# Running the low half of a causal score tile over all 128 rows of TensorE

## The chip, the cores and the metric

The kernel runs on one core of one Trainium2 chip. The metric is the device time of one execution in microseconds (us), taken as the median of several runs. A profile of one execution gives every instruction's start and duration on TensorE's matmuls (PE), TensorE's weight loads (PEld), VectorE (DVE), ScalarE (ACT), GpSimd (POOL) and the DMA issues of SyncE (SP).

## The reference

One decoder layer for 512 positions and 1024 channels in float32. Three mixers read the same normalised input: a gated short convolution, causal attention with 8 heads of 64 channels, and attention over 256 memory tokens. A gated merge, an output projection and an MLP with a convolution follow. The change lies in the causal attention, whose scores are

```python
qh = rmsnorm(q.reshape(bsz, s, h, 64), moba_q_gain)      # h = 8 heads of 64 channels
kh = rmsnorm(k.reshape(bsz, s, h, 64), moba_k_gain)
scores = einsum('qhd,khd->hqk', qh, kh) * 64 ** -0.5     # causal: key <= query
out = softmax(scores) @ vh                               # two blocks of 256: all earlier ones are selected
```

## The kernel before

Every product is made in a reduced float32 format of TensorE (float32r). To keep the accuracy, each operand is cut into a high part (ScalarE copies it into the reduced format) and a low part (VectorE subtracts the high part from the original). An ordinary product is then three matmuls into one PSUM bank, in `mm3` (L235 to L237): high times high, low times high, high times low. The weights arrive as 512 KB pieces of eight 128x128 blocks, through three buffers `raw` that SP loads (L180); ScalarE (L197, `hi`) and VectorE (L200, `lo`) cut them two pieces ahead of their use.

Most of the time goes into projections of 128x128 weight blocks against 512 positions. Attention runs beside them as background tasks: generators that emit their next step after a given number of half tiles (12 matmuls each) have passed on TensorE. TensorE's order is exactly the order of the program. For ScalarE, VectorE, GpSimd and SP a planner orders the instructions after the start of the kernel, from its own model of the times. The causal heads are spawned 7 or 8 half tiles apart.

Heads come in pairs p, because a tile of 128 channels holds two heads of 64. For a pair, the normalised queries are split once into high and low (L242 on ScalarE, L244 on VectorE). Three DMAs of 128 KB from SP (L677) then lay the high queries of head 0 into both halves of one tile and those of head 1 into both halves of another. The keys of a head go into one tile `k2` (written `k` in the profile's rows): the high keys on the head's own 64 partitions (L680), the low keys on the other 64 (L681). So one matmul over 128 rows sums high keys times high queries and low keys times high queries (L689). A second matmul adds high keys times low queries (L690): it uses only the head's own 64 rows of `k2` and of the tile of low queries.

The scores of a head are four tiles t of 128 keys, over 512, 384, 256 and 256 queries, in two banks of the tag "s". Two tiles are emitted, one half tile of other work is let pass, and then come the other two. ScalarE copies each out (L692); mask, maximum, exponential and split follow on GpSimd, VectorE and ScalarE. Six half tiles later the products with the values begin (L748): for two key tiles at a time, each with its high and its low probabilities, over the same 512, 384, 256 and 256 queries, all over 128 rows.

Tiles of queries and `k2` come from the tag "st" with 8 buffers; a buffer is free again when its last reader is done.

Of the kernel before, what the change touches and what calls it, by code (L numbers as in the profile page):

```python
# [26 lines left out]

# The start of the kernel: its pieces of work in the order in which ScalarE, VectorE and TensorE
# take them up.  Each word begins a piece or carries it on to its next step, mostly from its
# ScalarE half to its VectorE half.  c: cut weight piece; x, m: split chunk of x, of mem;  # L30
# q, n: add up its squares; R, N: row factors of x, of mem;
# Q: memory queries from a chunk of x; s: their row factors; K, V: memory keys, values;
# h: chunk of the normalised x; C: first projection of the conv mixer.
PLAN = """
# [7 lines left out]

# Packed per-channel vectors: name -> (first column, columns).
VEC = {}
# [10 lines left out]

# Column tiles of w_in.
T_B, T_C, T_X, T_Q, T_K, T_V, T_QM, T_G = 0, 4, 8, 12, 16, 20, 24, 28


def weight_units():  # L60
    """The 128x128 weight blocks (matrix, row chunk, column chunk) in the order of use."""
    u = []

    def inner(m, c, nk):
        u.extend((m, k, c) for k in range(nk))

    def outer(m, cs, nk):
        u.extend((m, k, c) for k in range(nk) for c in cs)

    outer("w_in", range(T_QM, T_QM + 4), KD)  # L70
    for c in range(4):
        inner("w_mem_kv", c, KD)
    outer("w_mem_kv", range(4, 8), KD)
    for c in range(4):
        for t in (T_C, T_X, T_B):
            inner("w_in", t + c, KD)
    for p in range(4):
        if p == 3:
            outer("w_in", range(T_V, T_V + 4), KD)
        inner("w_in", T_Q + p, KD)  # L80
        inner("w_in", T_K + p, KD)
    for g, m, ahead in ((0, "w_br_conv", 0), (2, "w_br_mem", 0), (1, "w_br_moba", AHEAD)):
        n = max(ahead, 1)
        for j in range(n):
            inner("w_in", T_G + 8 * g + j, KD)
        for j in range(8):
            inner(m, j, 4)
            if n + j < 8:
                inner("w_in", T_G + 8 * g + n + j, KD)
    outer("w_o", range(4), KD)  # L90
    for c in range(4, 8):
        inner("w_o", c, KD)
    outer("w_up", (0, NF, 1, NF + 1), KD)
    for f in range(2, NF):
        inner("w_up", f, KD)
        inner("w_up", NF + f, KD)
    outer("w_down", range(4), NF)
    for c in range(4, 8):
        inner("w_down", c, NF)
    return u  # L100
# [10 lines left out]
def layer_kernel(ctx: ExitStack, tc: tile.TileContext, xT, memT, vecs, ws, outT):  # L111
# [14 lines left out]
    def nm(s):  # L126
        count[0] += 1
        return f"{s}_{count[0]}"
# [8 lines left out]

# [1 line left out]
    warm = cp.tile([P, ML], FR, name="warm")  # L139
# [12 lines left out]

# [1 line left out]
    tasks = []  # L154
# [13 lines left out]

# [1 line left out]
    st = {"u": 0, "left": 0, "off": 0, "loaded": 0, "dram": 0, "cut": 0, "use": 0, "n": 0, "look": 0}  # L170
# [36 lines left out]
    def take(want, n=1):  # L207
        """The next n blocks (in one piece) as (high, low) parts."""
        for i in range(n):
            assert units[st["u"] + i] == want[i], (units[st["u"] + i], want[i])  # L210
        if st["left"] == 0:
            i = st["use"]
            st["use"] = i + 1
            while st["cut"] <= min(i + st["look"], len(sizes) - 1):
                cut_piece()
            while st["loaded"] < min(st["cut"] + 2, len(sizes)):
                load_piece()
            cuts.pop(i - 1, None)
            st["left"], st["off"] = sizes[i], 0
        assert st["left"] >= n  # L220
        hi, lo = cuts[st["use"] - 1]
        o = st["off"] * P
        st["off"] += n
        st["left"] -= n
        st["u"] += n
        return hi[:, o : o + n * P], lo[:, o : o + n * P]
# [25 lines left out]
    def split(dst, src, scale=None):  # L252
        """dst = (high, low) of src, or of src * scale."""
        for _ in split_steps(dst, src, scale):
            pass
# [23 lines left out]
    def fold(dst, src, op):  # L279
        """dst[32 a + j, b] = the 32 rows 32 a + i of src's column 32 b + j, put together."""  # L280
        nc.vector.tensor_reduce(  # L281
            dst, src.rearrange("p (b i) -> p b i", i=32), axis=AX.X, op=op, apply_transpose=True
        )

    def spread(dst, src):
        """dst[32 a + i, 32 b + j] = src[32 a + j, b]."""
        n = src.shape[-1]
        nc.vector.transpose(
            dst.rearrange("p (b i) -> p b i", i=32),
            src.unsqueeze(2).to_broadcast([src.shape[0], n, 32]),  # L290
        )

    def join_steps(part, op, width=P, act=True):
        """Put a fold's quadrants together, over all or over each half of the partitions."""
        def shift(n):
# [22 lines left out]
    def root_steps(w, v):  # L318
        """w = (v + EPS) ** -0.5: ScalarE's seed with a Newton step."""
        s = small(v.shape[-1])  # L320
# [15 lines left out]
    def row_steps(out, w, mean):  # L336
        """The row factors from the channels' shares of the mean squares."""
        part = small(mean.shape[-1] // 32)
# [8 lines left out]
    def head_norm(q, gain, wait):  # L347
        """RMS norm of q over the 128 channels of its head, in place."""
        n = q.shape[-1]
# [10 lines left out]

    # ================= mixers =================
    mid = ctx.enter_context(ExitStack())
# [4 lines left out]

# [1 line left out]
    start = ExitStack()  # L369
# [7 lines left out]

# [1 line left out]
    xr, mraw, xs = [], [], []  # L379
# [19 lines left out]
    rb = cp.tile([P, S], F32, name="rb")  # L399
    spots = [("st", 8)] * 8 + [("ph", 4)] * 3 + [("pl", 4)] * 3 + [("S", 2)] * 2  # L400
    spots = iter(spots)
# [4 lines left out]

    # The tensor engine's clock rises while it waits for the first loads.
    junk = bank("s")
# [118 lines left out]

# [1 line left out]
    y_mem = []  # L529

    def mem_head(i):
        qh = (
            sp.tile([P, S], FR, tag="st", name=nm("qmh"), bufs=8),
            sp.tile([P, S], FR, tag="st", name=nm("qml"), bufs=8),
        )
# [41 lines left out]

# [1 line left out]
    def conv3(u, w, b):  # L579
        """Causal width-3 taps over u, whose first two columns are the zero padding."""  # L580
        t = tmp()
# [6 lines left out]
    for c in range(4):  # L588
        # The first tile runs from x, whose row factors come in here, while h is finished.
        src = xs if c == 0 else hx  # L590
# [21 lines left out]

# [1 line left out]
    qkn = [[None, None] for _ in range(4)]  # L614
# [46 lines left out]

    # query columns that key tile t serves, and where they lie in a packed row
    OFF = (0, 512, 896, 1152)
    pairs, qs = {}, {}

    def moba_head(h):
        p, j = divmod(h, 2)
        own, oth = halves(j)
        kn = qkn[p][1][own, :]
        if j == 0:  # L670
            qs[p] = tuple(
                sp.tile([P, S], FR, tag="st", name=nm(n), bufs=8) for n in ("qh", "qh", "ql")
            )
            a, b, lo = qs[p]
            split((a, lo), qkn[p][0])
            for dst, src in ((b[own, :], a[oth, :]), (b[oth, :], a[oth, :]), (a[oth, :], a[own, :])):
                nc.sync.dma_start(dst.bitcast(F32), src.bitcast(F32))  # L677
        q_hi, q_lo = qs[p][j], qs[p][2][own, :]
        k2 = sp.tile([P, S], FR, tag="st", name=nm("k2"), bufs=8)
        nc.scalar.activation(k2[own, :], kn, AF.Copy)  # L680
# [3 lines left out]
        for t in range(4):  # L684
# [4 lines left out]
            nc.tensor.matmul(acc[:, :n], l, q_hi[:, q0:], start=True, stop=False)  # L689
            nc.tensor.matmul(acc[:, :n], l[own, :], q_lo[:, q0:], start=False, stop=True)  # L690
            w = S - P * t
# [77 lines left out]

# [1 line left out]
    merged = [None] * 8  # L771
# [60 lines left out]

# [1 line left out]
    x2, h2 = [], []  # L834
# [21 lines left out]

    # ================= MLP =================
    fp = ctx.enter_context(tc.tile_pool(name="fp", bufs=2 * NF))
# [36 lines left out]
    for c in range(4, 7):  # L895
        finish(proj_inner("w_down", c, mlp, tag="s"), c)
    # The last tile ends in two halves, so that less of it is left to store at the end.
    parts = [(bank(), slice(0, S // 2)), (bank(), slice(S // 2, S))]
# [61 lines left out]
```

## Time and profile before

| what | value |
|---|---|
| median of 3 runs | 856.29 us (854.37 to 857.18) |
| span of the profiled execution | 854.7 us |
| PE busy | 848.1 us (99%) in 3714 matmuls |
| PEld busy | 682.4 us (80%) in 3714 loads |
| DVE busy | 519.7 us (61%) |
| ACT busy | 381.3 us (45%) |
| POOL busy | 46.6 us (5%) |
| DMA moved | 86.19 MB, mean 101 GB/s |
| granted TensorE clock, mean | 0.998 of full speed |

The page of the profile gives the span of the profiled execution and no time of its own beside it; the span lies inside the range of the three runs. A busy share tells how long an engine had something in it: matmuls overlap in the array, so a matmul's duration is longer than the step from its start to the next one's start, and a PE that is busy throughout may still step slowly. The steps between starts are what to read.

### The profile page before, as it was taken

How to read it: one execution, taken by the hardware profiler on the slowest of the kernel's cores; microseconds unless marked ns; L12 is line 12 of the kernel's file. 1: busy time of each engine (PE TensorE's matmuls, PEld its weight loads, DVE VectorE, ACT ScalarE, POOL GpSimd, SP SyncE). 2: the span in 40 equal slices, each digit the busy share in tenths (PEclk: the TensorE clock that was granted, in tenths of full speed). 3: DMA queues.
4: the chain of work that ended last, by engine and by line, in shares of the span. 5: the costliest groups of instructions: out<-in, count | busy, mean ns of one | idle time of the engine just before them, and what ended most of it. 6: DMA issues, size and time to landing. Idle time of an engine off the chain costs nothing.

```text
span 854.7 us, 9970 instructions
## 1 busy us (share of the span) xinstructions
PE 848.1 (99%) x3714; PEld 682.4 (80%) x3714; DVE 519.7 (61%) x834; ACT 381.3 (45%) x682; POOL 46.6 (5%) x97
## 2 busy tenths in 40 slices
PE   9999999999999999999999999999999999999998
PEld 7788888877777777778888888888888888888888
DVE  5997898947756776656456666556655556323221
ACT  6666767736645654444334443333333333211110
POOL 0200000101211011110000000000000000000000
PEclk9999999999999999999999999999999999999999
DMA  8353222332322222225222222332223322233410
GB/s 297 116 173 104 79 96 78 109 101 75 93 75 93 99 74 79 73 81 187 98 99 98 80 94 99 99 98 83 91 99 98 99 99 79 94 99 120 139 62 25
DMA packets 25633, 86.19 MB, mean 101 GB/s; under 512 B 2928, under 2 KB 3568, under 8 KB 25456
## 3 DMA queue, kind: packets, MB, share of 16 engines
q1 hardware_dynamic: 25440, 85.47, 30.2%
q8 instruction: 29, 0.48, 0.2%
q14 instruction: 20, 0.16, 0.1%
q10 hardware_dynamic: 144, 0.08, 0.0%
HBM read 81.87 MB, written 2.10 MB: 98 GB/s over the span
## 4 chain that ended last, share of the span: by engine, by line
PE 95%; DVE 2%; DMA 2%; issue 0%; ACT 0%; SPq 0%; DVEq 0%; ACTq 0%
PE acc L235 25%; PE acc L237 24%; PE acc L236 24%; PE s L236 6%; PE s L237 6%; PE s L235 6%; PE s L690 1%; PE m L748 1%; DMA raw<-ws 1%; PE s L689 1%; DMA xr<-xT 1%; DVE mh L248 0%; DVE lo L200 0%; DVE ss_x L433 0%; PE m L237 0%
## 5 line engine op out<-in xcount | busy, mean ns | idle before, releaser
L200 DVE TENSOR_TENSOR lo<-raw,hi 128x1024 fp32r<-128x1024 f32 (+1 forms) x148 | 179.0, 1211 | 157.7 <-ACT hi L197 157.4
L197 ACT ACTIVATE hi<-raw 128x1024 fp32r<-128x1024 f32 (+1 forms) x148 | 154.9, 1047 | 267.9 <-PE acc L237 158.2
L235 PE MATMUL acc<-h,hi 128*128 128x512 f32 x568 | 225.6, 397 | 0.0
L237 PE MATMUL acc<-h,hi 128*128 128x512 f32 x568 | 224.3, 395 | 0.0
L236 PE MATMUL acc<-h,lo 128*128 128x512 f32 x568 | 224.2, 395 | 0.0
L235 PEld LDWEIGHTS acc<-h,hi 128*128 128x128 f32 x568 | 106.7, 188 | 26.5 <-issue 0.9
L237 PEld LDWEIGHTS acc<-h,hi 128*128 128x128 f32 x568 | 106.7, 188 | 25.7
L236 PEld LDWEIGHTS acc<-h,lo 128*128 128x128 f32 x568 | 106.8, 188 | 24.8
L236 PE MATMUL acc<-m,lo 128*128 128x512 f32 (+1 forms) x132 | 47.1, 357 | 0.0
L235 PE MATMUL acc<-m,hi 128*128 128x512 f32 (+1 forms) x132 | 47.1, 357 | 0.0
L237 PE MATMUL acc<-m,hi 128*128 128x512 f32 (+1 forms) x132 | 47.1, 357 | 0.0
L235 PE MATMUL s<-h,hi 128*128 128x512 f32 x112 | 44.2, 395 | 0.0
L236 PE MATMUL s<-h,lo 128*128 128x512 f32 x112 | 44.2, 395 | 0.0
L237 PE MATMUL s<-h,hi 128*128 128x512 f32 x112 | 44.2, 395 | 0.0
L300 ACT ACTIVATE ty<-ty 32x16 f32<-32x16 f32 (+4 forms) x136 | 29.1, 214 | 16.4 <-DVE ty L281 7.9
L869 ACT ACTIVATE tmp<-tmp 128x512 f32<-128x512 f32 x22 | 14.0, 635 | 41.2 <-DVE tmp L584 41.1
L867 DVE TENSOR_TENSOR u<-acc,r2b 128x512 f32<-128x512 f32 x15 | 10.4, 692 | 32.1 <-PE acc L237 32.1
L776 ACT ACTIVATE tmp<-acc,half_b 128x512 f32<-128x512 f32 x21 | 14.5, 689 | 33.8 <-PE acc L237 33.7
L235 PEld LDWEIGHTS acc<-m,hi 128*128 128x128 f32 x132 | 24.8, 188 | 4.1
L236 PEld LDWEIGHTS acc<-m,lo 128*128 128x128 f32 x132 | 24.8, 188 | 4.0
L237 PEld LDWEIGHTS acc<-m,hi 128*128 128x128 f32 x132 | 24.8, 188 | 4.0
L235 PE MATMUL s<-m,hi 128*128 128x512 f32 x66 | 26.1, 395 | 0.0
(218 smaller groups left out, 1370.2 us busy)
## 6 DMA issues: line engine op xcount, KB each, us to landing
raw<-ws SPq DMA_DIRECT2D x145, 512.0 KB, 3.3
xr<-xT SPq DMA_DIRECT2D x8, 256.0 KB, 5.0
xres<-xT SPq DMA_DIRECT2D x1, 2048.0 KB, 9.4
outT<-tmp SPq DMA_DIRECT2D x7, 256.0 KB, 3.7
qh<-qh SPq DMA_DIRECT2D x12, 128.0 KB, 2.2
mr<-memT SPq DMA_DIRECT2D x4, 256.0 KB, 8.3
raw<-ws SPq DMA_DIRECT2D x2, 128.0 KB, 3.2
raw<-ws SPq DMA_DIRECT2D x1, 256.0 KB, 4.7
```

Of the source, the lines that this page charges most:

```text
L197: nc.scalar.activation(hi[:, :m], raw[:, :m], AF.Copy)
L200: nc.vector.tensor_sub(lo[:, :m], raw[:, :m], hi[:, :m].bitcast(F32))
L235: nc.tensor.matmul(out, l[0], r[0], start=start, stop=False)
L236: nc.tensor.matmul(out, l[1], r[0], start=False, stop=False)
L237: nc.tensor.matmul(out, l[0], r[1], start=False, stop=stop)
L300: nc.scalar.activation(dst, src, AF.Copy)
L689: nc.tensor.matmul(acc[:, :n], l, q_hi[:, q0:], start=True, stop=False)
L690: nc.tensor.matmul(acc[:, :n], l[own, :], q_lo[:, q0:], start=False, stop=True)
L748: nc.tensor.matmul(acc[:, i0:], l, b[:, : S - i0], start=i == 0 and b is x[0], stop=i == 3 and b is x[1],)
L776: nc.scalar.activation(z, acc, AF.Tanh, bias=half_b[:, i : i + 1], scale=0.5)
L867: nc.vector.tensor_mul(u[:, 2 : S + 2], acc, r2b)
L869: nc.scalar.activation(t, t, AF.Silu)
```

## The change

The low queries get the same layout as the high ones: two tiles for a pair, in each of which one head's low queries lie on both halves of the partitions. Three more DMAs for each pair lay them there. The second matmul of each score tile then takes all 128 rows of `k2` (and so adds low keys times low queries as well). The tag "st" has 9 buffers in place of 8; a pair takes four tiles of queries and two of keys, where it took three and two.

```diff
         if j == 0:
             qs[p] = tuple(
-                sp.tile([P, S], FR, tag="st", name=nm(n), bufs=8) for n in ("qh", "qh", "ql")
+                sp.tile([P, S], FR, tag="st", name=nm(n), bufs=9)
+                for n in ("qh", "ql", "qh", "ql")
             )
-            a, b, lo = qs[p]
-            split((a, lo), qkn[p][0])
-            for dst, src in ((b[own, :], a[oth, :]), (b[oth, :], a[oth, :]), (a[oth, :], a[own, :])):
-                nc.sync.dma_start(dst.bitcast(F32), src.bitcast(F32))
-        q_hi, q_lo = qs[p][j], qs[p][2][own, :]
-        k2 = sp.tile([P, S], FR, tag="st", name=nm("k2"), bufs=8)
+            split(qs[p][:2], qkn[p][0])
+            for a, b in zip(qs[p][:2], qs[p][2:]):
+                for dst, src in (
+                    (b[own, :], a[oth, :]), (b[oth, :], a[oth, :]), (a[oth, :], a[own, :])
+                ):
+                    nc.sync.dma_start(dst.bitcast(F32), src.bitcast(F32))
+        q_hi, q_lo = qs[p][2 * j : 2 * j + 2]
+        k2 = sp.tile([P, S], FR, tag="st", name=nm("k2"), bufs=9)
...
             nc.tensor.matmul(acc[:, :n], l, q_hi[:, q0:], start=True, stop=False)
-            nc.tensor.matmul(acc[:, :n], l[own, :], q_lo[:, q0:], start=False, stop=True)
+            nc.tensor.matmul(acc[:, :n], l, q_lo[:, q0:], start=False, stop=True)
```

## Rows read from the trace of the kernel before

**Rows 1.** The page's chain that ended last: shares of the span by engine.

```profile
PE 95%; DVE 2%; DMA 2%; issue 0%; ACT 0%; SPq 0%; DVEq 0%; ACTq 0%
```

**Rows 2.** Windows: stretch, then busy us (instructions) by engine, granted clock, DMA share, GB/s.

```profile
190.00:285.00 95.00, 95.00 (x400) 73.61 (x400) 65.06 (x127) 55.33 (x118) 16.12 (x28) 1.00 0.28 90
```

**Rows 3.** Timeline of PE, head 0, score tiles 0 and 1: start us, duration us, instruction.

```profile
190.98 0.40 PE L236 MATMUL acc<-hi,h 128*128 128x512 f32 x1
191.21 0.40 PE L237 MATMUL acc<-lo,h 128*128 128x512 f32 x1
191.45 0.40 PE L689 MATMUL s<-qh,k 128*128 128x512 f32 x1
191.78 0.50 PE L690 MATMUL s<-ql,k 64*128 64x512 f32 x1
192.21 0.44 PE L689 MATMUL s<-qh,k 128*128 128x384 f32 x1
192.58 0.43 PE L690 MATMUL s<-ql,k 64*128 64x384 f32 x1
192.94 0.50 PE L235 MATMUL acc<-h,hi 128*128 128x512 f32 x1
193.28 0.39 PE L236 MATMUL acc<-h,lo 128*128 128x512 f32 x1
```

**Rows 4.** Timeline of PE, head 0, score tiles 2 and 3 (first and last).

```profile
195.82 0.28 PE L689 MATMUL s<-qh,k 128*128 128x256 f32 x1
...
197.30 0.39 PE L236 MATMUL acc<-h,lo 128*128 128x512 f32 x1
```

**Rows 5.** Timeline of PE, products with the values of head 0, and what follows each group.

```profile
213.87 0.40 PE L748 MATMUL m<-ph,v 128*128 128x512 f32 x1
...
214.68 0.39 PE L689 MATMUL s<-qh,k 128*128 128x512 f32 x1
...
219.05 0.28 PE L748 MATMUL m<-ph,v 128*128 128x256 f32 x1
...
219.52 0.28 PE L689 MATMUL s<-qh,k 128*128 128x256 f32 x1
```

**Rows 6.** Timeline of PE, head 7, score tiles 0 and 1 (first and last).

```profile
368.31 0.40 PE L689 MATMUL s<-qh,k 128*128 128x512 f32 x1
...
370.13 0.39 PE L236 MATMUL acc<-h,lo 128*128 128x512 f32 x1
```

**Rows 7.** Line L690, all its matmuls: minimum, median and maximum ns, first and last start.

```profile
L690 PE MATMUL s<-ql,k x32: 379/410/502, 191.8 to 373.5; 64*128 64x256 f32 x16, 64*128 64x512 f32 x8, 64*128 64x384 f32 x8
```

**Rows 8.** Timeline of PEld in the same stretch as rows 3.

```profile
190.98 0.19 PEld L237 LDWEIGHTS acc<-lo,h 128*128 128x128 f32 x1
191.22 0.19 PEld L689 LDWEIGHTS s<-qh,k 128*128 128x128 f32 x1
191.78 0.18 PEld L690 LDWEIGHTS s<-ql,k 64*128 64x128 f32 x1 [0.37 <-issue]
```

**Rows 9.** Timeline of SP's DMA issues: start us, us until the last was issued, count.

```profile
154.47 3.42 SPq L677 DMA_DIRECT2D qh<-qh  x3
...
223.03 5.50 SPq L677 DMA_DIRECT2D qh<-qh  x2
228.89 37.97 SPq L180 DMA_DIRECT2D raw<-ws  x7
271.53 3.42 SPq L677 DMA_DIRECT2D qh<-qh  x3
```

**Rows 10.** Chain in order of time, 150 to 380 us: second score matmuls of five heads.

```profile
215.07 0.43 PE s L690
...
241.97 0.42 PE s L690
...
246.22 0.31 PE s L690
...
292.09 0.42 PE s L690
...
341.81 0.43 PE s L690
```

**Rows 11.** Page, DMA issues: count, KB each, median us from issue to landing.

```profile
raw<-ws SPq DMA_DIRECT2D x145, 512.0 KB, 3.3
...
qh<-qh SPq DMA_DIRECT2D x12, 128.0 KB, 2.2
```

**Rows 12.** Timeline of ACT, cuts of four weight pieces (first and last).

```profile
219.25 1.06 ACT L197 ACTIVATE hi<-raw 128x1024 fp32r<-128x1024 f32 x1 [1.79 <-PE acc L237]
...
237.70 1.06 ACT L197 ACTIVATE hi<-raw 128x1024 fp32r<-128x1024 f32 x1 [0.31 <-PE acc L237]
```

**Rows 13.** Timeline of ACT, head 4: copying score tiles 0 and 1 out.

```profile
293.69 0.98 ACT L692 ACTIVATE S<-s 128x512 f32<-128x512 f32 x2
```

**Rows 14.** Timeline of PE, head 4, where score tiles 2 and 3 begin.

```profile
296.06 0.28 PE L689 MATMUL s<-qh,k 128*128 128x256 f32 x1
```

More of the change, by code (lines that the diff above doesn't have):

```diff
@@ L399, in layer_kernel @@
     rb = cp.tile([P, S], F32, name="rb")
-    spots = [("st", 8)] * 8 + [("ph", 4)] * 3 + [("pl", 4)] * 3 + [("S", 2)] * 2
+    spots = [("st", 9)] * 8 + [("ph", 4)] * 3 + [("pl", 4)] * 3 + [("S", 2)] * 2
     spots = iter(spots)
@@ L532, in mem_head @@
         qh = (
-            sp.tile([P, S], FR, tag="st", name=nm("qmh"), bufs=8),
-            sp.tile([P, S], FR, tag="st", name=nm("qml"), bufs=8),
+            sp.tile([P, S], FR, tag="st", name=nm("qmh"), bufs=9),
+            sp.tile([P, S], FR, tag="st", name=nm("qml"), bufs=9),
         )
```

## The prediction

> **What bounds the kernel now.** I read the chain that ended last first. TensorE holds 95% of the span [rows 1]; the rest is VectorE and DMA work at the kernel's start. So a change counts here if it shortens TensorE's own sequence, or if it makes TensorE wait. Next come the windows over the stretch in which the causal heads run: PE is busy for all of it at the full granted clock, while VectorE is busy for 65.06 of 95 us and ScalarE for 55.33 [rows 2]. Both have room. That busy figure hides TensorE's pace, because matmuls overlap, so third I read the timeline of PE by the steps from one start to the next.
>
> In an ordinary stretch a matmul of 512 columns starts 0.23 us after the one before it, though it lasts 0.40 [rows 3]. In the score tiles the steps are longer. From the first score matmul of 512 columns to the second (64 rows) 0.33 us pass; from that one to the next 128-row matmul 0.43; then 0.37 and 0.36 for 384 columns; and the first projection matmul afterwards, an ordinary one of 512 columns, takes 0.34 until its successor starts [rows 3]. The excess sits where the number of rows changes. The step into the first score matmul, from 128 rows to 128, is an ordinary 0.24. The weight loads show the same place: in the ordinary stretch a load starts together with the matmul before its own, 0.23 us ahead, whereas the 64-row load starts together with its own matmul, after 0.37 us in which the loading path had nothing to do [rows 8].
>
> **The change part by part.** *The second matmul on 128 rows.* The trace holds the same sequence of shapes without a change of rows. The products with the values run over 512, 512, 384, 384 columns and then over four times 256, all on 128 rows, each group adding into one bank. Their four steps take 214.68 - 213.87 = 0.81 us and 219.52 - 219.05 = 0.47 us [rows 5]. I compare from the first score matmul to the second projection matmul behind the tiles, since the last change of rows shows only there. For tiles 0 and 1 that is 193.28 - 191.45 = 1.83 us now [rows 3], and would be 0.81 + 0.23 = 1.04: 0.79 saved. For tiles 2 and 3 it is 197.30 - 195.82 = 1.48 [rows 4], and would be 0.47 + 0.23 = 0.70: 0.78 saved. Head 7 begins with 370.13 - 368.31 = 1.82 [rows 6], so the heads are alike. A head saves 1.57 us and eight save 12.6 us. By the other count, 32 matmuls of 64 rows [rows 7] make 64 changes of rows, 0.196 us each.
>
> Can a 128-row matmul itself cost more than a 64-row one? Its steps go by columns in rows 5, and I have only the sum above to compare, so the answer is in it. Ends: at best the sum plus the 0.02 by which steps in rows 3 vary, 32 times, 0.6 us more; at worst nothing is saved (the third rival).
>
> The page TensorE: Matmul & The Clock Gate of the Trainium skill, in its section "Why this matters for your kernels", says that a single matmul over few rows takes the same time as one over 128, and that few rows gain only when such matmuls run at once in different row groups. By that sentence alone the change would be worth 0 here, and the time would stay at the old one; by the rows it is worth 12.6 us, because what is paid is the change of rows and not the rows. I take the rows.
>
> *Twelve more DMAs of 128 KB.* Each lands 2.2 us after its issue [rows 11]. Exposed one after another they would cost 12 x 2.2 = 26 us; hidden, nothing. The high copies show which: those of pair 0 are issued by 157.9 (154.47 + 3.42), land by 160.1, and are first read at 191.45, 31 us later [rows 3, 9]. A second set, behind the first and as long, would land by 163.5. Pair 2's copies are out by 228.5 and pair 3's by 275.0 [rows 9], and heads 4 and 6 make their first second matmul at about 292 and 342 [rows 10]: over 60 us of cover. I take nothing.
>
> *What stands behind them on SP's queue.* SP issues in order, and the weight loads follow the copies. The third copy of a set waits for the first two to be read, which is why a set takes 3.42 us and not three issues in a row. A second set holds SP for another 3.4 us or so, for each pair. A weight load lands 3.3 us after issue [rows 11]. Three buffers mean that it goes out when the cut three pieces earlier is done: cuts stand at 219.25 and, three pieces later, 237.70 [rows 12]. Less the cut itself on ScalarE and VectorE (about 2.3 us) and the landing, nearly 13 us are left, and the cut piece is used two pieces, 2 x 24 x 0.23 = 11 us, after that. A hold of 3.4 us disappears in this. I take nothing.
>
> *Nine buffers in place of eight.* The queries and keys of two pairs in flight are 12 tiles, where they were 10. So where five tiles of a pair found 8 buffers, the fourth query tile of a pair may have to wait one head longer: the copies of pair 2 go out at 223 once head 1 is done, and head 2 is done only at about 247 [rows 9, 10]. Head 5, which reads that tile, comes some 70 us after that. It costs nothing by itself; what it can do to SP is a rival below.
>
> *ScalarE and VectorE.* No instruction is added to either. Four heads of this stretch lose 6.3 of 95 us, so VectorE's share rises from 65.06 / 95 = 68% to 65.06 / 88.7 = 73%. In the tightest place I found, ScalarE is done copying tiles 0 and 1 out at 294.67 (293.69 + 0.98) and the banks are wanted again from 296.06: 1.39 us to spare [rows 13, 14]. At most the 0.79 of one half comes off it. I take nothing.
>
> **Sum.** 854.7 - 12.6 = 842.1 us for an execution like the profiled one, 1.47% less. The median of the runs shown is 856.29, 0.19% above that span; scaled by it the forecast is 843.7 us.
>
> **The rivals.** *First, the score banks become the wait.* If ScalarE has a cut of 1.06 us ahead of the copy, the 0.6 us that remain of the spare time do not cover it: 0.45 us for each head, 3.6 in all, 847.3 us. For it: the planner orders ScalarE anew from its own model. Against it: 1.39 was the least spare time, and mostly ScalarE copies sooner.
>
> *Second, on the other side: SP stands still before a low copy.* The place is the copy into the fourth query tile. If the planner sets it in SP's order where the other three are ready, and the buffer comes free one head later, SP holds the weight loads for 247 - 223 = 24 us. The cover was 13 + 11 us less the 2.3 and 3.3 that a late piece still needs, about 19. TensorE would wait 5 us for each of the pairs 1 to 3, 15 us against 12.6 won: 843.7 + 15 = 858.7 us. It decides from a hold of some 23 us on; shorter holds only eat part of the gain. Against it: the planner has kept today's copies near their buffers' release, and rows 9 show holds of 3 to 6 us.
>
> *Third, nothing is gained.* Then the load of a 128-row matmul that follows another on the same bank would not run ahead, and its 0.19 us [rows 8] would stand in each of the 64 places: 64 x 0.19 = 12.2 of the 12.6 us are paid again, about 855.9 us. Against it: rows 5 have such groups without that cost, and in rows 8 a 128-row load runs beside a 128-row matmul. The page TensorE: Matmul & The Clock Gate of the Trainium skill, section "The mechanism" in its Part 3, states in its list that a weight load overlaps matmuls in flight only when it goes to another row group; by that rule this rival is the result, and the change removes the one overlap there is. Rows 8 disagree with the rule.
>
> **How the numbers follow.** Full gain, 843.7: 0.86. First rival, 847.3: 0.05. Third, 855.9: 0.04. Second, 858.7: 0.05. A difference of over 0.3% (2.6 us) is about what a measurement of this kernel can tell from no change. Faster by more: 0.86 + 0.05 = 0.91; within it 0.04; slower 0.05. The runs before spread over 2.8 us, 1.4 to a side, and the sum's upper end adds 0.6: the full gain alone covers 841.5 to 846. With the first rival and partial holds of SP the range is 841.0 to 847.5 us.
>
> **What would show it.** Right: every step in the score tiles is 0.23, 0.17 or 0.12 us as in rows 5, the loads of the second matmul begin beside the matmul before it, and the first half of a head to the second projection matmul takes 1.04 us. Twenty-four copies of queries, all landed tens of us before the heads that read them; weight pieces cut as early as now. Wrong: steps of 0.3 to 0.4 us remain on 128 rows (third rival); PE steps of a microsecond or more ahead of L689 that end with ScalarE's copy (first); SP holds of 20 us with PE waiting for a cut piece in the middle of a projection (second).

## The result, and the profile after

| | before | changed |
|---|---|---|
| median, us | 855.33 (852.22 to 857.18, 4 runs) | 842.88 (841.41 to 845.94, 4 runs) |
| ratio, 95% interval | | 0.9864 (0.9842 to 0.9886) |
| span of the profiled execution, us | 854.7 | 842.4 |

The kernel is 1.4% faster; 12.6 us were forecast, 842.1 us for the span and 843.7 for the time. The profiled execution of the changed kernel took 844.19 us, 1.8 more than its span. TensorE still sets the end. The page's chain that ended last, by engine:

```profile
PE 95%; DMA 2%; DVE 2%; issue 0%; ACT 0%; SPq 0%; DVEq 0%; ACTq 0%
```

The timeline of PE over the score tiles of head 0, which answers to [rows 3, 4] (start us, duration us, instruction; L693 and L694 are the two score matmuls):

```profile
190.98 0.40 PE L237 MATMUL acc<-lo,h 128*128 128x512 f32 x1
191.22 0.40 PE L693 MATMUL s<-qh,k 128*128 128x512 f32 x1
191.46 0.40 PE L694 MATMUL s<-ql,k 128*128 128x512 f32 x1
191.69 0.34 PE L693 MATMUL s<-qh,k 128*128 128x384 f32 x1
191.88 0.33 PE L694 MATMUL s<-ql,k 128*128 128x384 f32 x1
192.05 0.40 PE L235 MATMUL acc<-h,hi 128*128 128x512 f32 x1
192.28 0.40 PE L236 MATMUL acc<-h,lo 128*128 128x512 f32 x1
...
194.84 0.28 PE L693 MATMUL s<-qh,k 128*128 128x256 f32 x1
...
195.55 0.39 PE L236 MATMUL acc<-h,lo 128*128 128x512 f32 x1
```

The steps now go by the columns: 0.24 and 0.23 us for 512, 0.19 and 0.17 for 384. From the first score matmul to the second projection matmul the first half of the head takes 192.28 - 191.22 = 1.06 us where it took 1.83, and the second 195.55 - 194.84 = 0.71 where it took 1.48. The loads (PEld, same stretch, beside [rows 8]) are early again:

```profile
190.75 0.19 PEld L237 LDWEIGHTS acc<-lo,h 128*128 128x128 f32 x1
190.99 0.19 PEld L693 LDWEIGHTS s<-qh,k 128*128 128x128 f32 x1
191.23 0.19 PEld L694 LDWEIGHTS s<-ql,k 128*128 128x128 f32 x1
```

The load for L694 starts at 191.23, beside the matmul before it, where the 64-row load started only with its own matmul.

To see how much of the difference between the spans comes from this place, I take the stretch from the first score matmul to the last product with the values, 16 half heads in all. The line views give the first and last start. Before, the first score matmul is at 191.45 [rows 3], and the last product is the end of this row (minimum/median/maximum ns, first to last start):

```profile
L748 PE MATMUL m<-pl,v x32: 278/310/397, 214.1 to 394.7; 128*128 128x256 f32 x16, 128*128 128x512 f32 x8, 128*128 128x384 f32 x8
```

and of the changed kernel:

```profile
L693 PE MATMUL s<-qh,k x32: 278/310/402, 191.2 to 361.2; 128*128 128x256 f32 x16, 128*128 128x512 f32 x8, 128*128 128x384 f32 x8
L752 PE MATMUL m<-pl,v x32: 278/309/397, 212.3 to 382.2; 128*128 128x256 f32 x16, 128*128 128x512 f32 x8, 128*128 128x384 f32 x8
```

The stretch is 394.7 - 191.5 = 203.2 us before and 382.2 - 191.2 = 191.0 after: 12.2 of the 12.3 us by which the spans differ (the line view gives starts to 0.1 us). Nothing is given back later: from 100 us to its end the changed kernel has no step from one matmul's start to the next of over 0.24 us, where the score tiles had steps of up to 0.43.

### The profile page after: what moved, and what is told of

It reads as the page before. It is cut to its first block, busy times and chain, and to the rows that moved or that the text cites. A ratio compares the mean times of both kernels' runs of the same rounds, so it can differ in the third digit from the quotient of the medians.

```text
span 842.4 us, 9986 instructions
## 1 busy us (share of the span) xinstructions
PE 834.2 (99%) x3714; PEld 679.3 (81%) x3714; DVE 519.9 (62%) x834; ACT 380.8 (45%) x682; POOL 46.2 (5%) x97
## 4 chain that ended last, share of the span: by engine, by line
PE 95%; DMA 2%; DVE 2%; issue 0%; ACT 0%; SPq 0%; DVEq 0%; ACTq 0%
PE acc L237 25%; PE acc L236 25%; PE acc L235 25%; PE s L236 6%; PE s L237 6%; PE s L235 6%; PE m L752 1%; DMA raw<-ws 1%; PE s L693 1%; DMA xr<-xT 1%; PE s L694 1%; DVE lo L200 0%; DVE mh L248 0%; DVE ss_x L433 0%; PE m L237 0%
```

## The experiments

All ratios are to the kernel before, measured beside it. The causal heads begin up to 3 us apart from run to run (189.5 us with two halves, 192.8 with eight buffers), before the first score matmul. These two also differ in the mean granted clock from 20 to 40 and from 40 to 60 us: 1.00 and 1.00 with two halves, 0.89 and 0.94 with eight buffers; from 60 us on it is 1.00 in every profiled execution. So each run is read by the stretch just defined as well.

| run | changes of rows | median, us | ratio (95%) | stretch, us |
|---|---|---|---|---|
| before | 64 | 855.33 to 857.08 | | 203.2 |
| changed | 0 | 842.88 | 0.9864 (0.9842 to 0.9886) | 191.0 |
| grouped order | 32 | 850.22 | 0.9933 (0.9907 to 0.9959) | 196.9 |
| copies, 64 rows | 64 | 857.16 | 1.0015 (0.9998 to 1.0032) | 203.2 |
| eight buffers | 0 | 845.69 | 0.9870 (0.9841 to 0.9900) | 190.9 |
| all on 64 rows | 32 | 849.41 | 0.9923 (0.9900 to 0.9947) | 196.7 |
| two halves | 32, and 16 between halves | 845.10 | 0.9874 (0.9847 to 0.9901) | 192.3 |

**Grouped order: the same 64-row matmuls, half the changes.** The kernel before, with tiles 0 and 1 (then 2 and 3) worked side by side in their two banks:

```diff
-        for t in range(4):
...
-            nc.tensor.matmul(acc[:, :n], l, q_hi[:, q0:], start=True, stop=False)
-            nc.tensor.matmul(acc[:, :n], l[own, :], q_lo[:, q0:], start=False, stop=True)
+        for ts in ((0, 1), (2, 3)):
+            accs = []
+            for t in ts:
...
+                nc.tensor.matmul(accs[-1][:, : S - q0], l, q_hi[:, q0:], start=True, stop=False)
+            for t, acc in zip(ts, accs):
...
+                nc.tensor.matmul(acc[:, : S - q0], l[own, :], q_lo[:, q0:], start=False, stop=True)
```

> The kernel before, with the four matmuls of a half head in another order: both 128-row matmuls first (tile 0, tile 1), then both 64-row ones. The same 32 matmuls of 64 rows, but two changes of rows for each half head in place of four. Theory (each change of rows costs 0.196 us, the rows themselves nothing): 32 changes go, 6.3 us, span near 848.4 us, ratio to the kernel before near 0.993, and the step from one 64-row matmul to the next is an ordinary 0.23 us for 512 columns. Rival (the excess belongs to a 64-row matmul, 0.39 us each, whatever its neighbours): no change, 854.7 us, ratio 1.000.

Its timeline of PE, head 0 (x2 are two neighbours of 512 and 384 columns, merged):

```profile
190.41 0.57 PE L690 MATMUL s<-qh,k 128*128 128x512 f32 x2
190.91 0.67 PE L694 MATMUL s<-ql,k 64*128 64x512 f32 x2
191.51 0.50 PE L235 MATMUL acc<-h,hi 128*128 128x512 f32 x1
191.85 0.39 PE L236 MATMUL acc<-h,lo 128*128 128x512 f32 x1
```

and its line view:

```profile
L690 PE MATMUL s<-qh,k x32: 277/307/402, 190.4 to 365.8; 128*128 128x256 f32 x16, 128*128 128x512 f32 x8, 128*128 128x384 f32 x8
L754 PE MATMUL m<-pl,v x32: 274/310/397, 212.2 to 387.3; 128*128 128x256 f32 x16, 128*128 128x512 f32 x8, 128*128 128x384 f32 x8
```

The half head takes 191.85 - 190.41 = 1.44 us; 1.04 and two changes of 0.196 make 1.43. The stretch is 387.3 - 190.4 = 196.9 us, 6.3 less than before, by an order of instructions alone. The price follows the changes: the 32 matmuls of 64 rows are all still there, so the rival that puts 0.39 us on each of them falls. One detail was expected wrongly: the step from one 64-row matmul to the next is not the ordinary 0.23 us. The second one starts at 191.25 (inside the merged row), 0.34 after the first; a part of the change into 64 rows falls there. Nor does it matter that the two matmuls of a tile add into one bank: the change into 64 rows here goes from tile 1's bank to tile 0's, and the price is the same.

**Copies, 64 rows: the new layout without its use.** The changed kernel with one line put back:

```diff
-            nc.tensor.matmul(acc[:, :n], l, q_lo[:, q0:], start=False, stop=True)
+            nc.tensor.matmul(acc[:, :n], l[own, :], q_lo[own, q0:], start=False, stop=True)
```

> The changed kernel with its second matmul back on 64 rows: the twelve more copies, the four query tiles of a pair and the nine buffers stay. Theory (copies and buffers cost and bring nothing, all the gain is in the rows): as the kernel before, span 854.7 us, ratio 1.000 within 0.3%, 64 changes of rows of 0.196 us in the trace. Rival (a part of the gain or a hidden cost is in the layout or in the planner's new order): off by over 2.6 us either way.

Line view:

```profile
L693 PE MATMUL s<-qh,k x32: 276/389/444, 192.0 to 373.7; 128*128 128x256 f32 x16, 128*128 128x512 f32 x8, 128*128 128x384 f32 x8
L752 PE MATMUL m<-pl,v x32: 278/310/397, 214.6 to 395.2; 128*128 128x256 f32 x16, 128*128 128x512 f32 x8, 128*128 128x384 f32 x8
```

395.2 - 192.0 = 203.2 us, as before, and a ratio whose interval holds 1. Twelve more copies, a ninth buffer and the planner's new order neither cost nor bring anything that can be measured (the interval ends at 0.3%, the stretches agree to 0.1 us).

**Eight buffers: copies that wait longer.** The changed kernel with the tag "st" as it was:

```diff
-                sp.tile([P, S], FR, tag="st", name=nm(n), bufs=9)
+                sp.tile([P, S], FR, tag="st", name=nm(n), bufs=8)
```

(and so in the other places of the tag).

> The changed kernel with eight buffers of the tag st in place of nine, so that the query tiles of a pair wait longer for their buffers and the copies behind them too. Theory (copies have tens of microseconds to spare and the weight loads about 20): as the changed kernel, span near 842.4 us, ratio near 0.986, with holds of SP no longer than about 10 us. Rival (SP stands still before a copy and the weight pieces come late): PE waits for cut pieces, 5 us for each of three pairs, near 857 us, ratio 1.003.

Its timeline of SP (start us, us until the last was issued, count), from pair 2 on:

```profile
203.16 35.46 SPq L180 DMA_DIRECT2D raw<-ws  x7
243.96 1.11 SPq L681 DMA_DIRECT2D qh<-qh  x2
245.12 1.23 SPq L681 DMA_DIRECT2D ql<-ql  x2
...
252.61 37.21 SPq L180 DMA_DIRECT2D raw<-ws  x7
291.01 1.11 SPq L681 DMA_DIRECT2D qh<-qh  x2
```

and its line view:

```profile
L693 PE MATMUL s<-qh,k x32: 278/310/402, 192.8 to 362.7; 128*128 128x256 f32 x16, 128*128 128x512 f32 x8, 128*128 128x384 f32 x8
L752 PE MATMUL m<-pl,v x32: 278/309/397, 213.9 to 383.7; 128*128 128x256 f32 x16, 128*128 128x512 f32 x8, 128*128 128x384 f32 x8
```

All copies of pair 2 move to 244 us, those of pair 3 to 291, and the stretch stays at 383.7 - 192.8 = 190.9 us. The planner moves the copies behind weight loads in SP's order, and SP's longest wait for a buffer ahead of a copy is 5.4 us (from 140 to 380 us), within the 10 that were expected. The median lies 2.8 us above that of the changed kernel, within the spread of either, and the 1.5 us by which the two profiled spans differ (843.9 and 842.4) are there before the first score matmul (192.8 against 191.2).

**All on 64 rows: more of the 64-row matmuls, fewer changes.** The kernel before, one line:

```diff
-            nc.tensor.matmul(acc[:, :n], l, q_hi[:, q0:], start=True, stop=False)
+            nc.tensor.matmul(acc[:, :n], l[own, :], q_hi[own, q0:], start=True, stop=False)
```

> The kernel before with the first matmul of each score tile on the head's own 64 rows too; low keys times high queries is left out. 64 matmuls of 64 rows, but only two changes of rows for each half head (in and out). Theory (changes cost, rows do not): 32 changes go, 6.3 us, span near 848.4 us, ratio near 0.993, steps of 0.23, 0.17 and 0.12 us inside a half head. Rival (0.39 us belong to every 64-row matmul): 32 more of them, 12.5 us slower, near 867 us, ratio 1.015.

Its timeline of PE, head 0:

```profile
190.86 0.40 PE L237 MATMUL acc<-lo,h 128*128 128x512 f32 x1
191.19 0.49 PE L689 MATMUL s<-qh,k 64*128 64x512 f32 x1
191.53 0.39 PE L690 MATMUL s<-ql,k 64*128 64x512 f32 x1
191.76 0.34 PE L689 MATMUL s<-qh,k 64*128 64x384 f32 x1
191.94 0.34 PE L690 MATMUL s<-ql,k 64*128 64x384 f32 x1
192.21 0.50 PE L235 MATMUL acc<-h,hi 128*128 128x512 f32 x1
192.55 0.39 PE L236 MATMUL acc<-h,lo 128*128 128x512 f32 x1
```

and its line view:

```profile
L689 PE MATMUL s<-qh,k x32: 273/360/496, 191.2 to 366.8; 64*128 64x256 f32 x16, 64*128 64x512 f32 x8, 64*128 64x384 f32 x8
L690 PE MATMUL s<-ql,k x32: 274/306/394, 191.5 to 366.9; 64*128 64x256 f32 x16, 64*128 64x512 f32 x8, 64*128 64x384 f32 x8
...
L748 PE MATMUL m<-pl,v x32: 279/311/395, 212.9 to 387.9; 128*128 128x256 f32 x16, 128*128 128x512 f32 x8, 128*128 128x384 f32 x8
```

Between 64-row matmuls on the same half of the rows the steps are ordinary: 191.76 - 191.53 = 0.23 and 0.18. Each change shows in two parts: 0.10 us before the first matmul of the new kind starts (0.33 where 0.23 is ordinary) and again about 0.10 before the second one starts (0.34). The stretch is 387.9 - 191.2 = 196.7 us, 6.5 less, with twice as many 64-row matmuls. (The first 0.10 of the first change lies ahead of the stretch here.)

**Two halves: is it the number of rows, or which rows?** The changed kernel with

```diff
-            nc.tensor.matmul(acc[:, :n], l, q_hi[:, q0:], start=True, stop=False)
-            nc.tensor.matmul(acc[:, :n], l, q_lo[:, q0:], start=False, stop=True)
+            r = oth if t % 2 else own
+            nc.tensor.matmul(acc[:, :n], l[r, :], q_hi[r, q0:], start=True, stop=False)
+            nc.tensor.matmul(acc[:, :n], l[r, :], q_lo[r, q0:], start=False, stop=True)
```

> The changed kernel with both matmuls of a score tile on 64 rows: tiles 0 and 2 on the head's own half (high keys alone), tiles 1 and 3 on the other half (low keys alone). The rest of the scores is left out. Each half head has one change into 64 rows, one from one half of the rows to the other at 64 rows, and one back. Theory (what costs is a change in the number of rows): as the run with all score matmuls on 64 rows, 32 changes of 0.196 us, span near 848 us, and the step from tile 0 to tile 1 is an ordinary 0.23 us. Rival (any change of the rows in use costs): 48 changes, span near 851 us, and that step is 0.33 us or more. Third possibility (the two halves work side by side): matmuls of tile 1 start while those of tile 0 run, the four steps of a half head fall from 0.81 and 0.47 us towards half, up to 4.6 us less, span near 843.5 us.

Its timeline of PE, head 0:

```profile
189.20 0.40 PE L237 MATMUL acc<-lo,h 128*128 128x512 f32 x1
189.53 0.49 PE L694 MATMUL s<-qh,k 64*128 64x512 f32 x2
189.82 0.44 PE L695 MATMUL s<-ql,k 64*128 64x384 f32 x2
190.19 0.50 PE L235 MATMUL acc<-h,hi 128*128 128x512 f32 x1
190.53 0.40 PE L236 MATMUL acc<-h,lo 128*128 128x512 f32 x1
```

and its line view:

```profile
L694 PE MATMUL s<-qh,k x32: 381/410/496, 189.5 to 360.6; 64*128 64x256 f32 x16, 64*128 64x512 f32 x8, 64*128 64x384 f32 x8
...
L753 PE MATMUL m<-pl,v x32: 278/308/397, 210.7 to 381.8; 128*128 128x256 f32 x16, 128*128 128x512 f32 x8, 128*128 128x384 f32 x8
```

The program's order is tile 0 high, tile 0 low, tile 1 high, tile 1 low. The timeline has both high ones first, merged in one row, and both low ones behind them, with the shorter one, that of tile 1 (384 columns), in front. The four matmuls that took 192.21 - 191.19 = 1.02 us from the first to the next projection matmul take 190.19 - 189.53 = 0.66 here. That is tile 0's own two steps, 0.46, and the two parts of 0.10 that fall between these starts; tile 1's two matmuls add nothing. So a change of halves costs nothing that shows: the two halves work side by side. The third possibility held, and the stretch, 381.8 - 189.5 = 192.3 us, is 4.4 below that of the run with all on one half.

## Why the prediction was right

**The bound.** TensorE's own sequence was the bound, it was shortened, and nothing else became late (no step over 0.24 us from 100 us on): 12.2 us out of the stretch, 12.3 out of the span.

**The sum.** 12.6 us were forecast from the steps of two sequences of equal shapes, one with and one without changes of rows. The measured halves are 1.06 and 0.71 where 1.04 and 0.70 were taken from [rows 5]; 8 times 0.02 and 8 times 0.01 are 0.24 of the 0.4 us that are missing, and the rounding of the starts covers the rest. The saving is 12.2 / 64 = 0.191 us for each change where 0.196 was forecast, and 6.3 / 32 = 0.197 and 6.5 / 32 = 0.20 in the two runs that keep half of the changes.

**The rows cost nothing.** Grouped order and all on 64 rows show it together: the price stays the same for a given number of changes, whether 32 or 64 matmuls have 64 rows. The reading by which the change was worth 0 had the lone matmul right (0.23 us for 512 columns at 64 rows as at 128) and left out what it costs to enter and to leave. The Trainium skill says in TensorEngine Tiling (Array Packing), section "Key Properties", that a change of the tiling mode, and not just of the tile, drains TensorE. The runs agree on where a cost falls: 0.19 to 0.20 us for each change between 128 and 64 rows, and none for a step within 64 rows or from one half to the other. That the cost is a drain they do not show, since the ends of matmuls are modelled. What a change does inside TensorE stays open; the traces add only that the weight load across it starts together with its own matmul and not ahead of it, in [rows 8] as in the run with two halves (189.53).

**The third rival, that loads of 128-row matmuls do not run ahead,** fell with the changed kernel: the load for L694 starts at 191.23, beside a 128-row matmul that starts at 191.22. The rule in the list of the Trainium skill's page TensorE: Matmul & The Clock Gate (Part 3, "The mechanism") that was set against the forecast does not hold here: this load and this matmul both take all 128 rows.

**The copies cost nothing, but their cover was smaller than I wrote.** SP's timeline in the changed kernel, beside [rows 9]:

```profile
154.24 1.16 SPq L681 DMA_DIRECT2D qh<-qh  x2
155.50 1.19 SPq L681 DMA_DIRECT2D ql<-ql  x2
157.17 0.46 SPq L681 DMA_DIRECT2D qh<-qh  x1
158.50 0.46 SPq L681 DMA_DIRECT2D ql<-ql  x1
...
195.39 4.30 SPq L681 DMA_DIRECT2D ql<-ql  x3
...
242.44 1.11 SPq L681 DMA_DIRECT2D ql<-ql  x2
...
289.48 3.69 SPq L681 DMA_DIRECT2D ql<-ql  x3
295.78 85.87 SPq L180 DMA_DIRECT2D raw<-ws  x15
```

Pair 0's two sets are woven into each other and done 4.7 us after the first issue; no second 3.4 us are added. The low sets of pairs 1 to 3 take 3.3 to 4.3 us, about the 3.4 that were written. Of these pairs the whole low set, and not only the copies into the fourth tile, goes out a head later than the high one (289 for pair 3): the first two copies of a set write into its second tile, and the third waits for them. Pair 3's low set is issued by 293.2, and head 6 begins its scores at 332.0 (its first L693 in the timeline of PE), so some 39 us are left, less the landing, where I had written over 60. That was enough. The second rival's mechanism is there, since copies do wait for buffers, but the planner sets them near the release: SP's longest wait of this kind is 5.5 us, and 5.4 with eight buffers, against the 23 from which it would have decided.

**The score banks** lost more of their spare time than was bounded. In the changed kernel ScalarE's copies of head 4's tiles 0 and 1 (beside [rows 13])

```profile
287.32 0.98 ACT L696 ACTIVATE S<-s 128x512 f32<-128x512 f32 x2
```

are done at 288.30, and the next tiles, 2 and 3, begin at

```profile
288.94 0.28 PE L693 MATMUL s<-qh,k 128*128 128x256 f32 x1
...
289.17 0.28 PE L693 MATMUL s<-qh,k 128*128 128x256 f32 x1
```

By the prediction's count, to the start of tile 2, 0.64 us are left of 1.39. But that count mixes the two banks. Used in turn, they give tile 2 the bank of tile 0, which is free earlier; the copy that ends last frees the bank for tile 3. Before, tile 3 began at

```profile
296.58 0.38 PE L689 MATMUL s<-qh,k 128*128 128x256 f32 x1
```

1.91 us after the copies' end at 294.67. Now it is 289.17 - 288.30 = 0.87. So this bank lost 1.04 us and not at most 0.79, since the steps of tile 2 became shorter as well; it had more to lose than the prediction saw. The first rival did not come in; a further 0.9 us would bring it in at this place.

## What to carry to other kernels

On a TensorE that is busy throughout, read the steps between starts, and look for places where the number of rows changes: each change cost 0.19 to 0.20 us, with 256 columns as with 512, so a lone matmul on half the rows in a stream of full ones cost 0.39 us more than one on all rows. Fill the rows up if the operands can be had under cover (DMAs that are off the path), or, for half of the gain and without any copy, put the half-row matmuls next to each other. A sequence of the same shapes elsewhere in the same trace gives the time after such a change to a few hundredths of a microsecond.

## What the runs showed of the hardware that was not expected

Matmuls on the two halves of the rows, in different banks, ran side by side, which the expectation had only as its third possibility: in the run with two halves, both high matmuls began at 189.53, and TensorE began tile 1's before tile 0's second one, against the order of the program. In the scores as they must be computed, this brings nothing that I could work out: a tile needs three products over 64 rows, so by an estimate from these steps tiles 0 and 1 would take at best, with the work shared evenly between the halves, 3 x (0.23 + 0.17) / 2 = 0.60 us side by side and two changes of 0.196, 0.99 in all, against 0.81 with all rows. This was not run.
